# Four weight tiles loaded during the product ahead of a layer norm, and two Newton steps in scalar form

## The chip, the cores and the metric

The kernel runs on one core of one Trainium2 chip. The metric is the device time of one execution in microseconds (us), from start to end on that core; where several executions were taken, their median stands. The core's engines work through instruction queues of their own and meet at semaphores: TensorE (PE; its weight loads are listed as PEld), VectorE (DVE), ScalarE (ACT), GpSimd (POOL), and SyncE (SP), which here only issues DMAs.

## The reference

The program computes a block of a network on 512 tokens of width 1024 and then a second block with a state-space layer and a latent-attention layer. What matters here is the first block:

```python
x = layer_norm(x, ln_emb_g, ln_emb_b)
h = x @ w_in + b_in                      # then two kinds of attention: out_a, out_b
mix = concatenate([out_a, out_b]) @ w_o + b_o
x = layer_norm(DN_ALPHA * x + mix, ln1_g, ln1_b)
ca = memory_cross_attention(x, mem, xa_wq, ..., xa_wo, xa_bo)     # begins with x @ xa_wq
x = layer_norm(DN_ALPHA * x + ca, ln2_g, ln2_b)
f = square(relu(x @ w_up + b_up)) @ w_down + b_down
x = layer_norm(DN_ALPHA * x + f, ln3_g, ln3_b)
```

Everything is float32. A product of float32 accuracy is made of three TensorE products: each operand is split into a high part H and a low part L, and H·H, L·H and H·L are added up.

## The kernel before

Tokens are worked in four tiles of 128 (t = 0 to 3). Weights come in tiles of 128 x 1024 (512 KB). `wload` (L115) handles one: SP issues the DMA into a `wraw` tile, ScalarE copies it into `wh` (L121, the high part), and GpSimd subtracts the two in two halves into `wl` (L124, the low part). All of them lie in one pool, `wp`, with 3 buffers for `wraw` and 5 each for `wh` and `wl`; a buffer is given back when the last instruction that reads it is done.

`gemm_ln` (L559) makes a product and the layer norm behind it. It is called twice: with `w_o` for ln1 and with `xa_wo` for ln2. It opens a pool `lnp` for the norm, which holds gain, bias and small tiles, and runs `gemm_q` (L216): output token-major, in quarters of 256 columns; the first two quarters go over all tokens, the last two are done together, token tile by token tile, with four weight tiles held throughout (L242). After each token tile `ev` runs: L256 adds the residual and sums, L264 and L265 give the mean, L266 (ScalarE) the variance, `nrstd` (L98) one over the standard deviation, L268 and L269 scale and shift. Then the tile is put down (`defer`) for transposing: `xpose` (L272) lets TensorE transpose it (L279), ScalarE write the high part (L145) and VectorE the low part (L146).

`nrstd` starts from ScalarE's square root (L102) and VectorE's reciprocal (L104) and makes one Newton step in two instructions on a single column (L105, L106). It is called 28 times: four times each in the embedding norm, ln1, ln2, ln3 and three RMS norms.

Behind the product stands `gemm_lead` (L170): it loads the first four weight tiles of the next product (`xa_wq` behind ln1, `w_up` behind ln2), takes four PSUM banks and multiplies the first two token tiles (columns 0 to 255) by all four, and then the other two, while the last token tiles are still being normalised and transposed. After it L576 scales the normalised rows on VectorE for the next residual. The remaining tiles of that product are loaded by `gemm_s` through the same `wp` buffers.

The order of the instructions on each engine is not the order of the program text: a planner lists them by program order as priority and by the times at which, on its own model, an instruction's inputs and buffers are ready. On the chip each engine works through its list in order.

Of the kernel before, what the change touches and what calls it, by code (L numbers as in the profile page):

```python
# [8 lines left out]
F32R = mybir.dt.float32r  # L9
AF = mybir.ActivationFunctionType  # L10
ALU = mybir.AluOpType
AX = mybir.AxisListType
P = 128
# [11 lines left out]
class Net:  # L25
# [72 lines left out]
    def nrstd(self, pool, v, n, eps):  # L98
        nc = self.nc
        y = pool.tile([P, 2], F32, tag="nr", name=self.nm("nr"), bufs=4)  # L100
        y0, y1 = y[:, 0:1], y[:, 1:2]
        nc.scalar.activation(y0, v, AF.Sqrt, scale=4.0 / n, bias=self.eps[eps])  # L102
        nc.vector.tensor_scalar(v, v, 4.0 / n, 4.0 * eps, op0=ALU.mult, op1=ALU.add)
        nc.vector.reciprocal(y0, y0)  # L104
        nc.vector.scalar_tensor_tensor(y1, y0, v, y0, op0=ALU.mult, op1=ALU.mult)  # L105
        nc.vector.scalar_tensor_tensor(v, y1, -3.0, y0, op0=ALU.add, op1=ALU.mult)  # L106


    def nbcast(self, pool, key, n, eng=None):
# [2 lines left out]
        return t  # L112


    def wload(self, ap, n=1024, shape=None, leng=None):  # L115
        nc = self.nc
        raw = self.wp.tile([P, 1024], F32, tag="wraw", name=self.nm("wraw"), bufs=3)
        h = self.wp.tile([P, 1024], F32R, tag="wh", name=self.nm("wh"), bufs=5)
        l = self.wp.tile([P, 1024], F32R, tag="wl", name=self.nm("wl"), bufs=5)
        nc.sync.dma_start(raw[:, :n], ap)  # L120
        nc.scalar.activation(h[:, :n], raw[:, :n], AF.Copy)  # L121
        for o in range(0, n, 512):
            e = slice(o, min(n, o + 512))
            (leng or nc.gpsimd).tensor_tensor(l[:, e], raw[:, e], f32(h[:, e]), op=ALU.subtract)  # L124
        return h, l
# [41 lines left out]
            self.flush(n=1)  # L167


    def gemm_lead(self, aps, X, tags):  # L170
        XH, XL = X
        W = [self.wload(ap) for ap in aps]
        pss = [self.bank(tag) for tag in tags]
        for lo in (0, 256):
            q = slice(lo, lo + 256)
            for (wh, wl), ps in zip(W, pss):
                for k in range(8):
                    c = slice(k * P, (k + 1) * P)
                    self.mm3(ps[:, q], wh[:, c], wl[:, c], XH[:, k, q], XL[:, k, q], k == 0, k == 7)
                self.flush(n=1)  # L180
            self.flush()
        return pss


    def gemm_m(self, aps, nk, X, evac, nhs=2, nt=NT, tail=4, leng=None):
        XH, XL = X
        nc2 = nk // 2
        for nh in range(nhs):
# [13 lines left out]
            if tl:  # L202
                W = [self.wload(aps[nh * nc2 + c], leng=leng) for c in range(nc2 - tl, nc2)]
                for t in range(nt):
                    q = slice(t * P, (t + 1) * P)
                    for ci, (wh, wl) in enumerate(W):
                        for kk in range(2):
# [5 lines left out]

    def gemm_q(self, aps, nk, X, evac, tag="mm", tags=()):  # L216
        XH, XL = X
        tags = list(tags)
        bank = lambda: self.bank(tags.pop(0) if tags else tag)
        n4 = nk // 4  # L220
        tq = 2 if nk == 8 else 1

        def part(ps, qs, ts, W):
            first = True
            for y, qn in enumerate(qs):
                for k in range(nk):
                    wh, wl = W[y * n4 + k // 4]
                    n = slice((k % 4) * 256, (k % 4) * 256 + 256)
                    for i, t in enumerate(ts):
                        q = slice(t * P, (t + 1) * P)  # L230
                        o = (y + i) * 256
                        self.mm3(ps[:, o:o + 256], XH[:, k, q], XL[:, k, q], wh[:, n], wl[:, n], first, k == nk - 1)
                        first = False

        for qn in range(4 - tq):
            W = [self.wload(aps[qn * n4 + c]) for c in range(n4)]
            for ts in ((0, 1), (2, 3)):
                ps = bank()
                part(ps, (qn,), ts, W)
                for i, t in enumerate(ts):  # L240
                    evac(t, slice(qn * 256, qn * 256 + 256), ps[:, i * 256:i * 256 + 256], False)
        W = [self.wload(aps[(4 - tq) * n4 + c]) for c in range(tq * n4)]  # L242
        for t in range(NT):
            ps = bank()
            part(ps, range(4 - tq, 4), (t,), W)
            evac(t, slice(D - tq * 256, D), ps[:, :tq * 256], True)
            self.flush(keep=2)
# [42 lines left out]
    def block1(self, dbg):  # L290
        nc, a = self.nc, self.a
# [4 lines left out]
        xt = self.pair(R, [P, 8, T], "xa")  # L296
# [5 lines left out]
        lnp = lp.enter_context(self.pool("lnp"))  # L302
# [5 lines left out]
        W = [wk(0)]  # L308
# [32 lines left out]
        ap = ctx.enter_context(self.pool("attn"))  # L341
# [23 lines left out]
        ap = c3.enter_context(self.pool("small"))  # L365
# [9 lines left out]
        for c, nk in enumerate((3, 3, 2)):  # L375
            wh, wl = self.wload(a["win_m"][:, c * 984:c * 984 + nk * 328], n=nk * 328)
            for kk in range(nk):
                n = slice(kk * 328, (kk + 1) * 328)
# [79 lines left out]
        for n in range(1, NT):  # L458
            w = (n + 1) * P
            q = slice(n * P, (n + 1) * P)  # L460
            sc = scs[n] = tk.tile([P, w], F32, name=f"sc{n}")
            for h in range(8):
                ps = self.mm()
                x = iq[h % 2]
# [34 lines left out]
        mix = self.pair(R, [P, 8, T], "xa")  # L499
# [40 lines left out]
        self.rctx = ExitStack()  # L540
        self.res = self.res_tiles(self.rctx, load=True)
        xt = self.pair(self.Rb, [P, 8, T], "xb")
        self.pre = self.gemm_ln(a["w_o"], 8, mix, "ln1", "xa_bo", xt, lambda: self.gemm_lead([a["xa_wq"][i] for i in range(4)], xt, ("sc", "sc", "pv", "uv")), tags=('mm', 'mm', 'sc', 'sc', 'tr'))
        if self.stop == "ln1":
            for t in range(NT):
                dbg[f"r1_{t}"] = self.res[t]
# [9 lines left out]

    def gemm_ln(self, w, nk, X, ln, nbias, xt, nxt, tags=()):  # L559
        nc = self.nc  # L560
        with self.pool(self.nm("lnp")) as lnp:
            g = self.nbcast(lnp, ln + "_g", D)
            b = self.bcast(lnp, ln + "_b", D)
            bo = self.bcast(lnp, nbias, D)

            def ev(t, cs, ps, last):
                r = self.res[t]
                self.ln_part(lnp, t, r, ps, cs)
                if last:
                    self.ln_finish(lnp, t, r, g, b)  # L570
                    self.defer(lambda: self.xpose(r, xt, t, tag="tr"))
            self.gemm_q([w[i] for i in range(nk)], nk, X, ev, tags=tags)
            pre = nxt()
            if self.stop != ln:
                for r in self.res:
                    nc.vector.scalar_tensor_tensor(r, r, ALPHA, bo, op0=ALU.mult, op1=ALU.add)  # L576
        return pre
# [35 lines left out]
    def block1b(self, dbg):  # L613
        nc, a = self.nc, self.a
# [43 lines left out]
        ao = self.pair(self.Rb, [P, 8, T], "xb")  # L658
# [16 lines left out]
            S = nS  # L675
        ctx.close()
        x2 = self.pair(self.R, [P, 8, T], "xa")
        pre = self.gemm_ln(a["xa_wo"], 8, ao, "ln2", "b_down", x2, lambda: self.gemm_lead([a["w_up"][i] for i in range(4)], x2, ("sc", "sc", "pv", "pv")))
        if self.stop == "ln2":
            for t in range(NT):  # L680
                dbg[f"r2_{t}"] = self.res[t]
# [6 lines left out]
        nw = self.nbcast(fp, "norm_w0", D)  # L688
        u = None
        for hf in range(2):  # L690
# [11 lines left out]
            if hf == 0:  # L702
                self.banks(acc=4, mm=4)
                pre = ()
# [19 lines left out]
        W = self.gate0_w()  # L724
# [917 lines left out]
```

## Time and profile before

| what | us |
|---|---|
| median of 3 runs (lowest to highest) | 1715.33 (1712.84 to 1717.4) |
| profiled execution, its whole time | 1716.78 |
| its span, first to last instruction | 1714.8 |
| TensorE busy in it | 1657.8 (97%) |
| VectorE busy | 913.5 (53%) |
| ScalarE busy | 835.6 (49%) |
| GpSimd busy | 889.2 (52%) |

The shares are averages over very different stages. The granted clock of TensorE is 0.99 of full speed over the span. All times below are from the start of the span of the profiled execution. ln1 lies around 302 to 340, ln2 around 429 to 467, the embedding norm before 48, the third norm around 800 to 835. In a timeline row the first number is the start, the second the duration, `x2` the instructions merged in the row, and the bracket the engine's idle time before it and what ended it.

### The profile page before, as it was taken

How to read it: one execution, taken by the hardware profiler on the slowest of the kernel's cores; microseconds unless marked ns; L12 is line 12 of the kernel's file. 1: busy time of each engine (PE TensorE's matmuls, PEld its weight loads, DVE VectorE, ACT ScalarE, POOL GpSimd, SP SyncE). 2: the span in 40 equal slices, each digit the busy share in tenths (PEclk: the TensorE clock that was granted, in tenths of full speed). 3: DMA queues.
4: the chain of work that ended last, by engine and by line, in shares of the span. 5: the costliest groups of instructions: out<-in, count | busy, mean ns of one | idle time of the engine just before them, and what ended most of it. 6: DMA issues, size and time to landing. Idle time of an engine off the chain costs nothing.

```text
span 1714.8 us, 27158 instructions
## 1 busy us (share of the span) xinstructions
PE 1657.8 (97%) x10203; PEld 1477.9 (86%) x10203; DVE 913.5 (53%) x1965; ACT 835.6 (49%) x1694; POOL 889.2 (52%) x817
## 2 busy tenths in 40 slices
PE   6999999999999999999899999999999999999998
PEld 6877888889988888888878898889999888988998
DVE  7579763743663004402769877779221307667512
ACT  4455664453353124412558777776333426565532
POOL 6756433363374445543556777776544544344431
PEclk9999999999999999999999999999999999999999
DMA  8634313332232222222433333332434442123341
GB/s 286 201 104 130 105 50 114 127 111 78 96 111 98 86 98 93 92 98 78 145 107 99 99 110 100 105 112 86 148 110 136 137 132 66 54 69 97 107 142 50
DMA packets 68178, 187.20 MB, mean 109 GB/s; under 512 B 9968, under 2 KB 16544, under 8 KB 67792
## 3 DMA queue, kind: packets, MB, share of 16 engines
q1 hardware_dynamic: 50128, 152.95, 27.4%
q10 hardware_dynamic: 17632, 30.43, 5.6%
q8 instruction: 80, 1.31, 0.3%
q0 software_dynamic: 288, 2.10, 0.3%
q14 instruction: 50, 0.41, 0.1%
HBM read 163.86 MB, written 14.78 MB: 104 GB/s over the span
## 4 chain that ended last, share of the span: by engine, by line
PE 80%; DVE 10%; issue 3%; ACT 3%; DMA 2%; POOL 1%; ACTq 0%; DVEq 0%; SPq 0%; POOLq 0%
PE mm L129 15%; PE mm L131 15%; PE mm L130 15%; PE acc L130 5%; PE acc L131 5%; PE acc L129 5%; PE sc L130 2%; PE sc L131 2%; PE sc L129 2%; PE pv L130 1%; PE pv L131 1%; PE pv L129 1%; PE tr L887 1%; POOL wl L124 1%; DVE sc L479 1%
## 5 line engine op out<-in xcount | busy, mean ns | idle before, releaser
L124 POOL TENSOR_TENSOR wl<-wraw,wh 128x512 fp32r<-128x512 f32 (+1 forms) x498 | 658.0, 1346 | 509.7 <-ACT wh L121 477.4
L121 ACT ACTIVATE wh<-wraw 128x1024 fp32r<-128x1024 f32 (+4 forms) x254 | 258.5, 1019 | 409.6 <-PE acc L131 123.7
L129 PE MATMUL mm<-xaH,wh 128*128 128x512 f32 x552 | 221.2, 401 | 3.2 <-DVE qbL L140 1.3
L130 PE MATMUL mm<-xaL,wh 128*128 128x512 f32 x552 | 220.4, 399 | 0.0
L131 PE MATMUL mm<-xaH,wl 128*128 128x512 f32 x552 | 220.0, 399 | 0.0
L129 PE MATMUL mm<-wh,xaH 128*128 128x256 f32 x512 | 147.2, 288 | 1.4 <-ACT xaH L145 1.4
L130 PE MATMUL mm<-wl,xaH 128*128 128x256 f32 x512 | 145.6, 284 | 0.0
L131 PE MATMUL mm<-wh,xaL 128*128 128x256 f32 x512 | 145.2, 284 | 0.0
L129 PEld LDWEIGHTS mm<-xaH,wh 128*128 128x128 f32 x552 | 104.4, 189 | 27.2 <-DVE qbL L140 1.8
L131 PEld LDWEIGHTS mm<-xaH,wl 128*128 128x128 f32 x552 | 104.4, 189 | 23.7
L130 PEld LDWEIGHTS mm<-xaL,wh 128*128 128x128 f32 x552 | 104.5, 189 | 23.0
L878 POOL TENSOR_SCALAR S<-S,den 128x128 f32<-128x128 f32 (+1 forms) x96 | 50.9, 534 | 105.1 <-DVE den L877 89.0
L129 PEld LDWEIGHTS mm<-wh,xaH 128*128 128x128 f32 x512 | 97.8, 191 | 2.0 <-ACT xaH L145 1.8
L130 PEld LDWEIGHTS mm<-wl,xaH 128*128 128x128 f32 x512 | 97.7, 191 | 0.2
L131 PEld LDWEIGHTS mm<-wh,xaL 128*128 128x128 f32 x512 | 97.0, 190 | 0.1
L129 PE MATMUL mm<-wh,xbH 128*128 128x256 f32 x336 | 94.9, 283 | 0.7 <-DVE lnsum L256 0.5
L131 PE MATMUL mm<-wh,xbL 128*128 128x256 f32 x336 | 94.4, 284 | 0.1
L130 PE MATMUL mm<-wl,xbH 128*128 128x256 f32 x336 | 94.3, 282 | 0.0
L698 DVE TENSOR_TENSOR rl<-rl 128x512 f32<-128x512 f32 x32 | 43.7, 1366 | 78.4 <-ACT rl L697 78.4
L948 DVE SCALAR_TENSOR_TENSOR xbc<-mm,conv_w,xbc 128x511 f32<-128x511 f32 (+2 forms) x84 | 62.2, 741 | 11.6 <-ACT xbc L946 10.9
L876 ACT ACTIVATE S<-S,mx 128x128 f32<-128x128 f32 (+1 forms) x96 | 53.7, 560 | 24.2 <-DVE mx L875 22.1
L129 PEld LDWEIGHTS mm<-wh,xbH 128*128 128x128 f32 x336 | 63.6, 189 | 1.6 <-DVE lnsum L256 0.7
(633 smaller groups left out, 4747.4 us busy)
## 6 DMA issues: line engine op xcount, KB each, us to landing
wraw<-in_w_up SPq DMA_DIRECT2D x32, 512.0 KB, 3.3
wraw<-in_w_down SPq DMA_DIRECT2D x32, 512.0 KB, 3.2
wraw<-in_ssm_xbc SPq DMA_DIRECT2D x32, 512.0 KB, 3.3
Dm<-acd ACTq DMA_DIRECT2D x32, 256.0 KB, 3.2
wraw<-in_ssm_out SPq DMA_DIRECT2D x16, 512.0 KB, 3.5
wraw<-in_mla_z SPq DMA_DIRECT2D x16, 512.0 KB, 3.5
wraw<-in_mla_out SPq DMA_DIRECT2D x16, 512.0 KB, 3.6
wraw<-in_ssm_z SPq DMA_DIRECT2D x14, 512.0 KB, 3.3
```

The costliest lines, as they stand in the source:

```text
L121: nc.scalar.activation(h[:, :n], raw[:, :n], AF.Copy)
L124: (leng or nc.gpsimd).tensor_tensor(l[:, e], raw[:, e], f32(h[:, e]), op=ALU.subtract)
L129: mm(out, aH, bH, start=first, stop=False, skip_group_check=True)
L130: mm(out, aH, bL, start=False, stop=False, skip_group_check=True)
L131: mm(out, aL, bH, start=False, stop=last, skip_group_check=True)
L479: nc.vector.match_replace(out=scs[n], in_to_replace=m8, in_values=scs[n], imm_value=-3e38)
L698: nc.vector.tensor_tensor(r, r, r, op=ALU.mult)
L876: nc.scalar.activation(s, s, AF.Exp, bias=mx, scale=-1.0, accum_out=den)
L878: nc.gpsimd.tensor_scalar(s, s, den, 1.0, op0=ALU.mult, op1=ALU.mult)
L887: self.nc.tensor.transpose(pt[:, c], S[:, c], self.ident)
L948: nc.vector.scalar_tensor_tensor(o[:, j:], ps[:, :T - j], cw[:, m, 3 - j:4 - j], o[:, j:], op0=ALU.mult, op1=ALU.add)
```

## The change

Four things change. `nrstd`'s two Newton instructions become `tensor_scalar` with two column scalars in place of `scalar_tensor_tensor`. `wload` can take `wh` and `wl` from another pool, with 3 buffers there. `gemm_q` takes a function `ahead` and calls it when the last four weight tiles of its own product have been asked for, ahead of the loop over token tiles. `gemm_ln` passes one that loads the first four tiles of the next product, three of them into the norm's pool and the fourth into `wp`; `gemm_lead` gets them ready made. The arithmetic is the same.

```diff
-        nc.vector.scalar_tensor_tensor(y1, y0, v, y0, op0=ALU.mult, op1=ALU.mult)
-        nc.vector.scalar_tensor_tensor(v, y1, -3.0, y0, op0=ALU.add, op1=ALU.mult)
+        nc.vector.tensor_scalar(y1, y0, v, y0, op0=ALU.mult, op1=ALU.mult)
+        nc.vector.tensor_scalar(v, y1, -3.0, y0, op0=ALU.add, op1=ALU.mult)
...
-    def wload(self, ap, n=1024, shape=None, leng=None):
+    def wload(self, ap, n=1024, leng=None, pool=None):
         nc = self.nc
         raw = self.wp.tile([P, 1024], F32, tag="wraw", name=self.nm("wraw"), bufs=3)
-        h = self.wp.tile([P, 1024], F32R, tag="wh", name=self.nm("wh"), bufs=5)
-        l = self.wp.tile([P, 1024], F32R, tag="wl", name=self.nm("wl"), bufs=5)
+        h, l = ((pool or self.wp).tile([P, 1024], F32R, tag=x, name=self.nm(x), bufs=3 if pool else 5) for x in ("wh", "wl"))
...
-    def gemm_lead(self, aps, X, tags):
+    def gemm_lead(self, aps, X, tags, W=None):
         XH, XL = X
-        W = [self.wload(ap) for ap in aps]
+        W = W or [self.wload(ap) for ap in aps]
...
-    def gemm_q(self, aps, nk, X, evac, tag="mm", tags=()):
+    def gemm_q(self, aps, nk, X, evac, tag="mm", tags=(), ahead=None):
...
         W = [self.wload(aps[(4 - tq) * n4 + c]) for c in range(tq * n4)]
+        if ahead:
+            ahead()
         for t in range(NT):
...
-    def gemm_ln(self, w, nk, X, ln, nbias, xt, nxt, tags=()):
+    def gemm_ln(self, w, nk, X, ln, nbias, xt, nw, lead, tags=()):
...
-            self.gemm_q([w[i] for i in range(nk)], nk, X, ev, tags=tags)
-            pre = nxt()
+            W = []
+            self.gemm_q([w[i] for i in range(nk)], nk, X, ev, tags=tags, ahead=lambda: W.extend(self.wload(nw[i], pool=lnp if i < 3 else None) for i in range(4)))
+            pre = self.gemm_lead(None, xt, lead, W)
```

The two calls of `gemm_ln` pass the weights (`a["xa_wq"]`, `a["w_up"]`) and the bank tags in place of the function that called `gemm_lead`.

## Rows read from the trace of the kernel before

**Rows 1.** The page: busy time, share of the span and instructions.
```profile
PE 1657.8 (97%) x10203; PEld 1477.9 (86%) x10203; DVE 913.5 (53%) x1965; ACT 835.6 (49%) x1694; POOL 889.2 (52%) x817
```

**Rows 2.** TensorE's waits, whole span: who, released by: us in total, times, longest.
```profile
PE mm L279 <- DVE res L330: 4.7, 2, 4.4
PE sc L130 <- DVE xbL L146: 4.0, 1, 4.0
...
PE sc L130 <- DVE lnmu L264: 2.7, 1, 2.7
...
PE z L131 <- DVE lnmu L265: 1.2, 1, 1.2
```

**Rows 3.** Windows: length, busy PE, PEld, DVE, ACT, POOL, granted clock, DMA share, GB/s.
```profile
318.00:323.20 5.20, 0.96 (x6) 0.55 (x4) 5.20 (x9) 1.49 (x3) 5.20 (x4) 0.99 0.61 202
323.20:326.40 3.20, 3.17 (x15) 3.17 (x16) 3.20 (x3) 1.79 (x4) 2.06 (x3) 0.50 0.49 163
...
452.80:456.10 3.30, 3.30 (x18) 3.30 (x17) 3.27 (x5) 1.54 (x3) 3.30 (x3) 0.50 0.43 159
```

**Rows 4.** Timeline of VectorE behind ln1.
```profile
310.75 0.69 DVE L256 CUSTOM_DVE_ANT_0 res<-mm,res 128x512 f32<-128x512 f32 x1 [0.62 <-PE mm L131]
...
313.02 1.22 DVE L576 SCALAR_TENSOR_TENSOR res<-res,xa_bo 128x1024 f32<-128x1024 f32 x1
...
317.38 0.69 DVE L256 CUSTOM_DVE_ANT_0 res<-mm,res 128x512 f32<-128x512 f32 x1 [0.62 <-PE mm L131]
...
317.99 1.10 DVE L105 SCALAR_TENSOR_TENSOR nr<-nr,lnvar 128x1 f32<-128x1 f32 x1
...
319.08 2.29 DVE L576 SCALAR_TENSOR_TENSOR res<-res,xa_bo 128x1024 f32<-128x1024 f32 x1
321.30 1.21 DVE L106 SCALAR_TENSOR_TENSOR lnvar<-nr 128x1 f32<-128x1 f32 x1
322.44 0.14 DVE L265 TENSOR_SCALAR lnmu<-lnmu 128x1 f32<-128x1 f32 x1
322.50 1.27 DVE L146 TENSOR_TENSOR xbL<-tr,xbH 128x512 fp32r<-128x512 f32 x2
```

**Rows 5.** Timeline of GpSimd around ln1.
```profile
296.41 5.04 POOL L124 TENSOR_TENSOR wl<-wraw,wh 128x512 fp32r<-128x512 f32 x4 [1.54 <-ACT wh L121]
...
315.12 8.62 POOL L124 TENSOR_TENSOR wl<-wraw,wh 128x512 fp32r<-128x512 f32 x6 [12.65 <-ACT wh L121]
```

**Rows 6.** Timeline of ScalarE behind ln1.
```profile
317.81 1.09 ACT L145 ACTIVATE xbH<-tr 128x512 fp32r<-128x512 f32 x2 [0.70 <-PE tr L279]
```

**Rows 7.** Timeline of VectorE behind ln2.
```profile
446.58 2.30 DVE L268 SCALAR_TENSOR_TENSOR res<-res,lnmu,ln_g 128x1024 f32<-128x1024 f32 x1 [2.48 <-ACT jk L266]
...
449.55 1.54 DVE L576 SCALAR_TENSOR_TENSOR res<-res,b_down 128x1024 f32<-128x1024 f32 x1
451.01 0.68 DVE L146 TENSOR_TENSOR xaL<-tr,xaH 128x512 fp32r<-128x512 f32 x1
```

**Rows 8.** Timeline of ScalarE around ln2.
```profile
442.87 1.06 ACT L121 ACTIVATE wh<-wraw 128x1024 fp32r<-128x1024 f32 x1 [0.79 <-PE mm L131]
```

**Rows 9.** Timeline of GpSimd around ln2.
```profile
444.01 12.90 POOL L124 TENSOR_TENSOR wl<-wraw,wh 128x512 fp32r<-128x512 f32 x8 [17.08 <-ACT wh L121]
```

**Rows 10.** Timeline of VectorE in the embedding norm.
```profile
24.52 1.24 DVE L105 SCALAR_TENSOR_TENSOR nr<-nr,mv 128x1 f32<-128x1 f32 x1
...
30.41 2.28 DVE L330 SCALAR_TENSOR_TENSOR res<-res,mv,ln_emb_b 128x1024 f32<-128x1024 f32 x1
```

**Rows 11.** Timeline of VectorE in the third norm.
```profile
818.47 1.31 DVE L105 SCALAR_TENSOR_TENSOR nr<-nr,lnvar 128x1 f32<-128x1 f32 x1
819.71 0.68 DVE L146 TENSOR_TENSOR xaL<-mm,xaH 128x512 fp32r<-128x512 f32 x1
```

**Rows 12.** Instructions on the tile lnvar: duration ns min/median/max, first and last start.
```profile
L105 DVE SCALAR_TENSOR_TENSOR nr<-nr,lnvar x12: 210/220/1315, 307.1 to 826.3; 128x1 f32<-128x1 f32 x12
...
L269 DVE SCALAR_TENSOR_TENSOR res<-res,lnvar,ln_b x12: 1269/1284/2367, 307.5 to 827.8; 128x1024 f32<-128x1024 f32 x12
```

More of the change, by code (lines that the diff above doesn't have):

```diff
@@ L542, in block1 @@
         xt = self.pair(self.Rb, [P, 8, T], "xb")
-        self.pre = self.gemm_ln(a["w_o"], 8, mix, "ln1", "xa_bo", xt, lambda: self.gemm_lead([a["xa_wq"][i] for i in range(4)], xt, ("sc", "sc", "pv", "uv")), tags=('mm', 'mm', 'sc', 'sc', 'tr'))
+        self.pre = self.gemm_ln(a["w_o"], 8, mix, "ln1", "xa_bo", xt, a["xa_wq"], ("sc", "sc", "pv", "uv"), tags=('mm', 'mm', 'sc', 'sc', 'tr'))
         if self.stop == "ln1":
@@ L677, in block1b @@
         x2 = self.pair(self.R, [P, 8, T], "xa")
-        pre = self.gemm_ln(a["xa_wo"], 8, ao, "ln2", "b_down", x2, lambda: self.gemm_lead([a["w_up"][i] for i in range(4)], x2, ("sc", "sc", "pv", "pv")))
+        pre = self.gemm_ln(a["xa_wo"], 8, ao, "ln2", "b_down", x2, a["w_up"], ("sc", "sc", "pv", "pv"))
         if self.stop == "ln2":
```

## The prediction

> **What bounds the kernel now.** I read the page first: TensorE is busy for 97% of the span [rows 1], so only what shortens its pauses, or the stretches in which it runs at half clock, can move the end. The list of its waits names the pauses that this change can reach [rows 2]: 4.4 us in the embedding norm, until L330 has written a token tile; 4.0 us behind the first layer norm (ln1) and 2.7 us behind the second (ln2), both until L146 has written the low half of the second token tile, which the first products read; 1.2 us in the third norm. (The last two rows name L264 and L265, one-element steps that stand next to L146 on VectorE; it is L146 that TensorE needs.) The windows then show that the pauses behind ln1 and ln2 are each followed by some 3.2 us at a granted clock of 0.50, 1.2 instead of 2.4 GHz [rows 3]; half of that, 1.6 us, is lost as well.
>
> Why is L146 late? Behind ln1 ScalarE writes its half from 317.81 on, the first of two parts by 318.4 [rows 6], so L146 could begin there. It begins at 322.50 [rows 4]. In between VectorE runs L105, one element per partition, in 1.10 us instead of 0.22 [rows 12]; L576 in 2.29 us instead of the 1.22 of the one at 313.02; L106, again one element, in 1.21; and L265, 0.14 us. All this time GpSimd splits weights without a break [rows 5]. The row of L265 is the telling one: a TENSOR_SCALAR of one element is not held up, a SCALAR_TENSOR_TENSOR of one element is held up for about one GpSimd instruction, and so is the big one. L146 itself, with one operand in PSUM, isn't: 1.27 us for two. Behind ln2 the same queue stands with other members: L268 at 2.30 us and L576 at 1.54 us ahead of L146, and no Newton step [rows 7].
>
> **The Newton steps (L105, L106)**, 28 calls. Unhindered, L105 falls from 0.22 to about 0.14 us, the length of L265; in nearly all calls that lies under TensorE's products. On the path stands the last call of all: -0.1 us. Four places where a step was held up count.
> Embedding norm: L105 at 24.52 takes 1.24 us and delays what follows it by 1.1; L330, at the end of the chain, runs 2.28 us from 30.41 [rows 10]. Begun 1.1 us earlier it may also meet GpSimd at a better moment, so TensorE gains between 0 and 1.6 us; but GpSimd's splits then wait for VectorE in turn and feed the next products, so I take -1.0.
> Behind ln1: L105 and L106 ahead of L146 lose 0.95 and 1.06 us, so L146 comes 2.0 us earlier, other things equal.
> Behind ln2: none stands ahead of L146: 0.
> Third norm: an L105 of 1.31 us stands ahead of the second L146 at 819.71 [rows 11]; TensorE's pause there, 1.2 us, can go. But GpSimd's queue of splits is not shorter for it: the next large VectorE instruction meets the split that the small one met before. Between 0 and -1.4; I take -0.6.
> The one-element TENSOR_SCALAR in the rows has constants for its scalars [rows 4]; one with columns in memory does not occur, so this is the nearest row, and the old hold of up to 1.1 us stays as the other bound. The Trainium skill, SBUF — State Buffer, section "Who interferes with whom", counts tensor_scalar among the operations that can take the port pair shared with GpSimd, in a two-port mode, besides instructions with two SBUF inputs. By that the new form could wait as the old one does, and this part would bring 0; the row of L265, 0.14 us with GpSimd busy, speaks against it for one element.
>
> **The four weight tiles.** Each is one DMA on SP's queue, one ScalarE copy (L121, 1.06 us [rows 8]) and two GpSimd subtractions (L124; 5.04 us for four, so 1.26 each [rows 5]). None of this is removed. The order on SP's queue stays: the product's tiles, then these four. Before, one of the four found a free buffer; the other three waited until the product gave its last buffers back, which is why ScalarE copies the second tile behind ln2 at 442.87, released by a product, L131 [rows 8]. With three tiles in the norm's pool that wait is gone, and they can be split in the 12.65 us (ln1) and 17.08 us (ln2) in which GpSimd stood idle [rows 5, 9]; the 7.6 us of six subtractions fit there.
> Was TensorE waiting for these weights? No: neither of its long waits behind the two norms names L121 or L124 [rows 2]. So the move brings nothing by itself. Its use would be an idle GpSimd while VectorE prepares L146. Here I had to choose. The buffers that the product gives back during its last token tile are now free for the *next* weights of the following product, and the planner refills a buffer as soon as it and a landed tile are there: before, eight subtractions ran in one go behind ln2, four tiles, one more than the three that were waiting [rows 9]. So I expect the fifth to seventh tile to be split just where the second to fourth were, and L576, L268 and L269 to be held up as before.
> What the move adds is hold-ups earlier. Ahead of L576 at 313.02 VectorE runs L268 and L269 for the first two token tiles, four two-input instructions of 1.28 us. One that meets a split is held up by 1.0 us (2.30 against 1.28 [rows 7, 12]). VectorE has 0.62 us idle twice to absorb it [rows 4]. All four met: 4 x 1.0 - 1.24 = +2.8 us; none: 0. I take three: +1.8. Against the 2.0 of the Newton steps ln1 comes out at -0.2. Its bounds: the pause gone (322.50 back to 318.4, -4.1) with the clock's -1.6, and +2.8.
> Behind ln2 the early splits lie in the idle 17.08 us before 444.01, and VectorE has 2.48 us idle before its critical queue [rows 7], which covers two meetings. So 0; with that cover gone +1.5 at most, and -2.7 - 1.6 if the pause goes.
> ScalarE's queue is the other place to look at: the copies now stand, in order, ahead of the norm's L266 of the first tiles, and a copy that waits for its DMA holds L266 and with it L268. The first two token tiles have time to spare, since TensorE transposes each of them a whole tile's product later: 0, bound +1.4 (one L121 and a piece of a landing). On GpSimd's queue L111, which L268 needs, is issued first. The 24 KB more in the norm's pool lie on tiles that the attention has left, and what comes to lie on them later is written after the first products' last read: 0.
>
> **The sum.** -0.1 - 1.0 - 0.2 + 0 - 0.6 = -1.9 us. The profiled execution took 1716.78 us, 1714.8 of it span; that would be 1712.9 of span and 1714.9 in all. On the median of 1715.33, which is what is compared, it is 1713.4 us, 0.11% less. Under 0.3%, 5.1 us, a measurement of this kernel can hardly tell a change from none.
>
> **The rivals.**
> *The gap closes (faster).* If the freed buffers are refilled later, GpSimd is idle while L146 is due. Behind ln1 L105, L576, L106 and L265 then take 1.7 us in place of 4.5 (-2.8), behind ln2 L268 and L576 take 1.28 + 1.22 in place of 2.30 + 1.54 (-1.3), and the clock may stay at 1.00 (2 x -1.6). With the other terms' -1.7 that is -9.0: 1706.3 us; with L576 behind L146 it would go down to 1703.6. For it: the held-up instructions are there in the rows. Against it: the fourth tile in one go [rows 9]. Chance 0.20. Half of it, 2.0 behind ln1 and no fall of the clock there, is 2.0 + 1.6 + 1.7 = 5.3 less, 1710.0 us; chance 0.15.
> *A longer queue on VectorE (slower).* The early splits meet all four instructions of the first two tiles, the freed buffers are refilled at once, and VectorE comes late to its critical queue; it decides from a backlog over the 2.0 us that the Newton steps give back. With ln1 at +2.8 and its 2.0 spent on new meetings, ScalarE's wait at +1.4, ln2 at +1.5 and one more stretch at the low clock, +1.6, less 1.7, it is +5.6: 1720.9 us. For it: from 318 to 326.4 VectorE does not pause at all [rows 3]. Against it: the idle spots before, and an early start of the splits. Chance 0.12.
> *The new form waits too.* Then the Newton terms are gone and ln1 stays at +1.8: 1717.1 us, within 0.3%. Chance 0.08.
>
> **How the numbers follow.** My own case has 0.45, at 1713.4, from 1710.5 to 1717.5. Within 0.3% are it and the last rival: 0.53. Faster by over 0.3%: 0.20 + 0.15 = 0.35. Slower: 0.12. The two outer cases reach beyond their times; 1703.5 to 1720.0 leaves out some 0.08 below and 0.11 above.
>
> **What would show it.** Right: L105 and L106 as TENSOR_SCALAR at about 0.14 us even where GpSimd is busy; the second to fourth tile's L121 ahead of the second token tile's L266; GpSimd still splitting when the last token tile's L256 ends; a pause of 3 to 5 us behind ln1 and of about 2.7 us behind ln2, each with 0.50 after it; the pause at L330 about 1 us shorter. Wrong: GpSimd idle in those two places and L146 right behind L145 (the first rival); L268 or L269 of the first two tiles at 2.3 us and L146 behind ln1 over 5 us after the last L256 (the second); L105 over 0.5 us anywhere (the third). The planner also orders every queue anew; if VectorE's order behind the norms changes, say L576 behind L146, the terms no longer hold.

## The result, and the profile after

| kernel | median us (lowest to highest, runs) | against before, 95% interval |
|---|---|---|
| before | 1715.26 (1712.84 to 1717.68, 6) | |
| changed | 1732.15 (1727.6 to 1732.64, 6) | 1.0091 [1.008, 1.0101] |

The change makes the kernel slower by 0.91%, 16.9 us; the prediction was 1713.4 us, 0.11% faster. The profiled execution took 1731.1 us, 1729.1 of it span, 14.3 more than before. Line numbers move by one or two: L121 is L120 now, L124 L123, L145 and L146 L144 and L145, L256 L257, L268 and L269 L269 and L270, L576 L578.

The page of the changed kernel: busy time by engine. TensorE is busy 7.5 us longer for the same number of instructions [rows 1], as it runs longer at half clock (the windows below); the other half of the loss is pauses.

```profile
PE 1665.3 (96%) x10203; PEld 1484.1 (86%) x10203; DVE 909.1 (53%) x1965; ACT 835.9 (48%) x1694; POOL 896.8 (52%) x817
```

The list of TensorE's waits in the changed kernel: who, released by what, us in total, times, longest.

```profile
PE tr L280 <- DVE xbL L145: 5.1, 1, 5.1
PE sc L129 <- DVE lnmu L265: 4.3, 2, 2.7
PE mm L128 <- DVE xaL L139: 4.2, 1, 4.2
PE mm L280 <- DVE res L331: 3.5, 2, 2.9
...
PE py L1051 <- DVE y L1068: 2.1, 1, 2.1
```

Three of these are new against [rows 2]: the first (ahead of the second token tile's transposes, ln1), the third (behind the first products of ln1) and the last (state-space stage). The pause in the embedding norm fell from 4.4 to 2.9 us, though in `e5_first_in_wp` below, with the same Newton form, it is 4.6; the one behind ln2 is still 2.7; the one behind ln1 is 1.6 now, with the 5.1 ahead of it.

Windows of the changed kernel (columns as in [rows 3]): the new pause at ln1, what follows it, the new pause behind the first products, what follows it, and the stretch behind ln2.

```profile
314.20:319.50 5.30, 0.27 (x3) 0.06 (x1) 5.30 (x5) 2.34 (x4) 5.24 (x3) 0.95 0.39 138
318.90:329.10 10.20, 7.97 (x35) 7.47 (x36) 9.48 (x20) 3.68 (x6) 6.19 (x5) 0.50 0.44 154
...
350.40:354.80 4.40, 0.28 (x3) 0.07 (x1) 2.12 (x3) 4.15 (x6) 3.02 (x2) 0.80 0.00 0
353.10:359.90 6.80, 5.05 (x12) 3.99 (x13) 5.15 (x7) 3.86 (x6) 2.16 (x1) 0.50 0.54 184
458.90:465.70 6.80, 5.69 (x26) 5.69 (x27) 6.69 (x13) 1.76 (x4) 6.80 (x4) 0.50 0.43 154
```

Before, ln1 had 3.2 us at 0.50 [rows 3], and there was nothing at 350 (a window of the kernel before, same columns):

```profile
345.00:360.00 15.00, 15.00 (x82) 12.84 (x81) 7.88 (x7) 7.61 (x10) 13.37 (x9) 1.00 0.57 185
```

Cut at the last TensorE instruction ahead of pauses that these kernels share, the span compares like this (the third column is the kernel with the Newton steps alone, below):

| stretch, up to | before | changed | Newton alone |
|---|---|---|---|
| the pause at xaH ahead of ln1's product | 291.0 | 288.2 | 287.2 |
| the first wait for S in the cross attention | 86.7 | 97.9 | 84.6 |
| the pause behind ln2 | 71.0 | 71.0 | 71.0 |
| the wait for dts, start of the state-space stage | 407.0 | 407.7 | 407.9 |
| the wait for X in that stage | 319.5 | 324.4 | 319.2 |
| the end of the span | 539.6 | 540.1 | 539.2 |

The sum is +14.3, and two rows carry it: +11.2 from ln1 to the cross attention, +4.9 in a stage that the change doesn't touch. ln2, the other place with early tiles, shows nothing.

What happens at ln1. GpSimd and VectorE of the changed kernel, timelines:

```profile
301.53 20.86 POOL L123 TENSOR_TENSOR wl<-wraw,wh 128x512 fp32r<-128x512 f32 x12 [3.49 <-DMA wraw<-in_xa_wq]
```
```profile
303.14 2.02 DVE L269 SCALAR_TENSOR_TENSOR res<-res,lnmu,ln_g 128x1024 f32<-128x1024 f32 x1
...
306.33 2.32 DVE L270 SCALAR_TENSOR_TENSOR res<-res,lnvar,ln_b 128x1024 f32<-128x1024 f32 x1
308.58 2.31 DVE L269 SCALAR_TENSOR_TENSOR res<-res,lnmu,ln_g 128x1024 f32<-128x1024 f32 x1
...
311.55 0.26 DVE L105 TENSOR_SCALAR nr<-nr,lnvar 128x1 f32<-128x1 f32 x1
...
312.10 2.28 DVE L270 SCALAR_TENSOR_TENSOR res<-res,lnvar,ln_b 128x1024 f32<-128x1024 f32 x1
314.30 2.29 DVE L578 SCALAR_TENSOR_TENSOR res<-res,xa_bo 128x1024 f32<-128x1024 f32 x1
316.51 2.28 DVE L269 SCALAR_TENSOR_TENSOR res<-res,lnmu,ln_g 128x1024 f32<-128x1024 f32 x1
318.72 1.27 DVE L145 TENSOR_TENSOR xbL<-tr,xbH 128x512 fp32r<-128x512 f32 x2
```

GpSimd, which before stood idle for 12.65 us here [rows 5], now runs twelve subtractions in one piece, and each of VectorE's six large instructions with two SBUF operands meets one: 2.02 to 2.32 us instead of 1.28. From the first L269 to L145 of the *first* token tile, at 318.72, it takes 15.6 us; before, the same six took 9.7, from 305.61 to 315.35 (VectorE of the kernel before, the first of the six and the low half of the first token tile):

```profile
305.61 1.28 DVE L268 SCALAR_TENSOR_TENSOR res<-res,lnmu,ln_g 128x1024 f32<-128x1024 f32 x1
...
315.35 1.28 DVE L146 TENSOR_TENSOR xbL<-tr,xbH 128x512 fp32r<-128x512 f32 x2
```

L145 has to read the two PSUM banks of that tile before TensorE can transpose the second tile into them. So TensorE stops not behind the first products, where the prediction looked, but ahead of the transposes.

What happens at 350. ScalarE and SP's queue of the changed kernel:

```profile
350.65 1.06 ACT L120 ACTIVATE wh<-wraw 128x1024 fp32r<-128x1024 f32 x1 [12.37 <-PE uv L129]
351.61 1.04 ACT L144 ACTIVATE xcH<-kvraw 128x1024 fp32r<-128x1024 f32 x1
352.56 1.25 ACT L138 ACTIVATE xaH<-sc,xa_bq 128x512 fp32r<-128x512 f32 x2
```
```profile
319.95 6.24 SPq L119 DMA_DIRECT2D wraw<-in_xa_wo  x3
328.19 2.30 SPq L623 DMA_DIRECT2D kvraw<-kd  x2
```

The four first products end one after another in four PSUM banks; each could be evacuated (L138, L139) when it is done. But ScalarE idles 12.37 us: at the head of its queue stands a weight copy, L120, of `xa_wo`, the product *after the next*. Its raw tile was fetched from 319.95 on, and it waits for the buffer that the last of the four first products (`uv`) reads. All four evacuations stand behind it, and the next product needs the banks and what is written from them: 4.2 us of pause, and 6.8 us at half clock that begin inside it.

### The profile page after: what moved, and what is told of

Same layout as the page of the kernel before. It is cut to its first block, busy times and chain, and to the rows that moved or that the text cites. A ratio compares the mean times of both kernels' runs of the same rounds, so it can differ in the third digit from the quotient of the medians.

```text
span 1729.1 us, 27155 instructions
## 1 busy us (share of the span) xinstructions
PE 1665.3 (96%) x10203; PEld 1484.1 (86%) x10203; DVE 909.1 (53%) x1965; ACT 835.9 (48%) x1694; POOL 896.8 (52%) x817
## 4 chain that ended last, share of the span: by engine, by line
PE 78%; DVE 13%; ACT 3%; issue 2%; DMA 2%; POOL 1%; ACTq 0%; DVEq 0%; SPq 0%; POOLq 0%
PE mm L128 14%; PE mm L129 14%; PE mm L130 14%; PE acc L129 5%; PE acc L130 5%; PE acc L128 5%; PE sc L129 2%; PE sc L130 2%; PE sc L128 2%; PE pv L129 2%; PE pv L130 1%; PE pv L128 1%; DVE xbc L950 1%; DVE sc L480 1%; DVE m L479 1%
## 5 line engine op out<-in xcount | busy, mean ns | idle before, releaser
L123 POOL TENSOR_TENSOR wl<-wraw,wh 128x512 fp32r<-128x512 f32 (+1 forms) x498 | 666.2, 1363 | 523.3 <-ACT wh L120 490.6
L120 ACT ACTIVATE wh<-wraw 128x1024 fp32r<-128x1024 f32 (+4 forms) x254 | 258.7, 1019 | 419.5 <-PE acc L130 125.7
L130 PEld LDWEIGHTS mm<-wh,xaL 128*128 128x128 f32 x512 | 97.9, 192 | 0.1
```

What stands on the lines that cost most here:

```text
L130: mm(out, aL, bH, start=False, stop=last, skip_group_check=True)
```

## The experiments

All ratios are against the kernel before, run beside each group on the same chip; the medians of before were 1715.62, 1715.30, 1717.11 and 1717.31 us for the four groups in order.

### One part alone

The first four kernels take the change apart. `e1_newton` is the kernel before with the two tensor_scalar lines. `e2_move` is the change with

```diff
-        nc.vector.tensor_scalar(y1, y0, v, y0, op0=ALU.mult, op1=ALU.mult)
-        nc.vector.tensor_scalar(v, y1, -3.0, y0, op0=ALU.add, op1=ALU.mult)
+        nc.vector.scalar_tensor_tensor(y1, y0, v, y0, op0=ALU.mult, op1=ALU.mult)
+        nc.vector.scalar_tensor_tensor(v, y1, -3.0, y0, op0=ALU.add, op1=ALU.mult)
```

`e3_ln1` and `e4_ln2` pass `ahead` only for the one norm, and load the four tiles in `gemm_lead` for the other:

```diff
-self.gemm_q(..., ahead=lambda: W.extend(...))
+self.gemm_q(..., ahead=lambda: W.extend(...) if ln == "ln1" else None)
-pre = self.gemm_lead(None, xt, lead, W)
+pre = self.gemm_lead([nw[i] for i in range(4)], xt, lead, W)
```

> The kernel before with the two Newton steps in scalar form and nothing else. Theory A (the splits that are now early hold up VectorE's queue at ln1; the Newton form is a small gain): in the changed kernel the work ahead of ln1 came 2.9 us earlier, and L105 and L106 behind ln1 lost 2.0 us before; so 2 to 5 us less than before, 1710 to 1713.5 us. Rival B (the loss is that of an order that the planner makes anew, whatever is edited): the stretch behind ln2, which this edit touches no more than the whole change does, shows the +5 us that it lost in the changed kernel, and the time is 1717 to 1721 us. Rival C (one-element tensor_scalar with column scalars, 0.26 us in place of 0.22, costs): within 1 us of 1715.3.

> The change with the old form of the Newton steps: the four weight tiles alone are moved. Theory A: the whole loss and what the Newton form had given back, 1733 to 1737 us; L105 and L106 at 1.1 to 2.3 us each where GpSimd splits without a break behind ln1. Rival C: 1730 to 1732 us, no worse than the whole change.

> The whole change at ln1, the four tiles loaded as before at ln2. Theory A: ln1 lost 11.2 us up to the first products of ln2, ln2 about 1, and the rest of the loss came further on; so 1722 to 1728 us, with a TensorE pause of about 5 us ahead of the transposes of the second token tile and one of about 4 us behind the first products. Rival B: what is lost further on (5 us between 864 and 1189 us) hangs on the planner's order and not on ln2, so it is there too or has another sign: 1728 to 1733 or under 1720 us.

> The whole change at ln2, the four tiles loaded as before at ln1. Theory A: ln1 keeps only the gain of the Newton steps (2 to 5 us less), ln2 adds 0 to 2 us, the longer stretch at half clock behind it 1.7: 1712 to 1717 us. Rival B: the 5 us of the later stretch stay: 1717 to 1722 us.

| kernel | median us | ratio, 95% interval |
|---|---|---|
| e1_newton | 1713.27 | 0.9982 [0.9969, 0.9996] |
| e2_move | 1726.71 | 1.0069 [1.0046, 1.0092] |
| e3_ln1 | 1730.22 | 1.009 [1.0064, 1.0115] |
| e4_ln2 | 1713.66 | 0.9991 [0.9977, 1.0004] |

The Newton steps are a small gain, the tiles at ln1 the whole loss, the tiles at ln2 about 0.1%, within the error. `e3_ln1` is 2 us above what theory A gave, and where rival B put it, since the loss of the state-space stage came with it (324.8 us) though ln2 is as before. `e2_move` missed both of its ranges: the move without the Newton steps should have been slower than the whole change, and is faster by about 5 us. Its stretch from ln1 to the cross attention is nearly as long as the whole change's (96.9 us); the difference lies in the state-space stage, 317.0 us against 324.4. That belongs to the last part of this section.

How fine the stretches can be read is shown by `e3_ln1` too. From ln1 to the cross attention it runs the same instructions in the same order as the changed kernel, on TensorE, VectorE, ScalarE and GpSimd, and takes 95.6 us where that one takes 97.9: its pause ahead of the transposes is 4.3 us, not 5.1, and behind the pause of 4.2 us it runs 3.4 us at half clock, not 6.8. Each stretch is from one execution, so a difference of some 2 us between two of them can be chance.

Behind ln1, `e1_newton` shows the queue that the prediction had in mind for the Newton term (VectorE's timeline; in this kernel the old line numbers hold):

```profile
314.14 0.27 DVE L105 TENSOR_SCALAR nr<-nr,lnvar 128x1 f32<-128x1 f32 x1
...
314.40 2.02 DVE L576 SCALAR_TENSOR_TENSOR res<-res,xa_bo 128x1024 f32<-128x1024 f32 x1
316.34 0.20 DVE L106 TENSOR_SCALAR lnvar<-nr 128x1 f32<-128x1 f32 x1
316.46 0.68 DVE L146 TENSOR_TENSOR xbL<-tr,xbH 128x512 fp32r<-128x512 f32 x1
```

L146 starts 2.3 us after L105 instead of 4.5 [rows 4]. What is left of the queue is L576.

### The early splits

`e8_no_split` leaves out GpSimd's subtractions for the four tiles at ln1; DMAs, copies and buffers stay. `e6_early` keeps them but asks for three of the tiles one quarter of the product earlier:

```diff
         for qn in range(4 - tq):
+            if ahead and qn:
+                ahead()
             W = [self.wload(aps[qn * n4 + c]) for c in range(n4)]
```

> The whole change, but the four tiles at ln1 are not split: no subtraction on GpSimd for them, and the products read the high part in place of the low part. Their DMAs, ScalarE copies and buffers stay, so the output isn't the reference's. Theory A1: with GpSimd's eight subtractions away, L269 and L270 of the first two token tiles take 1.28 us and the pause ahead of the second token tile's transposes goes; 5 to 9 us less than the changed kernel, 1723 to 1727 us. Rival (ScalarE's copies, in order ahead of the norm's square, are what makes VectorE late): the pause of 4 us and more stays, 1730 us and over.

> The whole change, with three tiles asked for one quarter earlier (ahead of the second quarter of the product, where VectorE does little) and the fourth behind the product, in the common pool. Theory A1 (the splits beside the norm of the first two token tiles cost the 5 us ahead of the second token tile's transposes): GpSimd is idle again from about 302 to 315 us, L269 and L270 of the first two tiles take 1.28 us, and the pause ahead of the transposes goes: 5.2 us and half of the 6.8 us more at half clock; the pause at 350 stays: 1721 to 1725 us. Rival (the three buffers more, not the splits' place, cost: the tiles that are refilled run beside the norm in any case): a pause of 4 us and more ahead of those transposes stays, 1729 us and over.

`e8_no_split`: 1724.46 us, 1.0047 [1.0031, 1.0064], as theory A1 had it. GpSimd (the first row: its timeline) is idle again as before, and the pause ahead of the transposes is gone; VectorE's L272, the L270 of the change, takes 1.29 us in the middle case (second row: the instructions on the tile res from 301 to 326 us, ns as minimum, median and maximum).

```profile
312.95 13.57 POOL L125 TENSOR_TENSOR wl<-wraw,wh 128x512 fp32r<-128x512 f32 x7 [13.10 <-ACT wh L120]
```
```profile
L272 DVE SCALAR_TENSOR_TENSOR res<-res,lnvar,ln_b x3: 1285/1286/2103, 307.7 to 321.0; 128x1024 f32<-128x1024 f32 x3
```

The copies are all there, so ScalarE's copies are not what makes VectorE late; the splits are. The stretch falls from 97.9 to 89.0 us. The pause of 4.3 us behind the first products stays, as it should.

`e6_early`: 1750.53 us, 1.0201 [1.0183, 1.0219], a miss by 25 us. The pause ahead of the transposes is gone here too, but its list of TensorE's waits has two new ones, both at the second quarter of a product, of ln1's and of ln2's:

```profile
PE sc L128 <- ACT wh L120: 10.5, 1, 10.5
...
PE mm L128 <- ACT wh L120: 6.8, 1, 6.8
```

The early tiles take the three `wraw` buffers and the queues ahead of the product's own weights. The expectation had counted only where the splits run, not the loads that they push back.

### The copy at the head of ScalarE's queue

`e5_first_in_wp` puts the first of the four tiles, not the fourth, into the common pool (`pool=lnp if i else None`), so that the buffer comes free three products earlier. `e9_hold` keeps the change and puts a holder between: one buffer of the weight pool is taken by an instruction that can only run once the fourth bank is evacuated, so no copy of `xa_wo` can stand ahead of the evacuations.

```diff
         ao = self.pair(self.Rb, [P, 8, T], "xb")
+        hold = self.wp.tile([P, 1024], F32R, tag="wh", name=self.nm("wh"), bufs=5)
+        nc.scalar.activation(hold[:, 0:2], f32(qT[0][:, 3, 0:2]), AF.Copy)
```

> The whole change, with the first of the four tiles in the common pool and the other three in the norm's pool (changed kernel: the fourth in the common pool). Theory A2 (the pause of 4.3 us behind the first products of ln1 comes from ScalarE's queue: a copy of a later weight tile waits there for the buffer that the last of the first products gives back, and the evacuation of the four banks stands behind it): the buffer now comes free with the first of these products, the pause at 350 goes, and the 6.8 us at half clock behind it: 1722 to 1727 us. Rival (the evacuation is late because VectorE and GpSimd are behind by what ln1 lost): the pause stays, over 3 us, 1730 to 1733 us.

> The whole change, and one tile of the weight pool is taken, ahead of the weights of the product after next, by an instruction of two elements that reads the fourth evacuated bank: no copy of those weights can then stand ahead of the evacuations in ScalarE's queue. Theory A2 (narrowed: what the freed buffers let come early is the loading of xa_wo, the product after next; its DMAs and copies wait for buffers at the head of SP's and ScalarE's queues, and the k/v loads and the evacuations stand behind them): the pause at 350 falls below 1.5 us and the half clock behind it goes: 1723 to 1728 us. Rival (VectorE and the k/v data are late by themselves): the pause stays over 3 us, 1730 to 1734 us.

`e5_first_in_wp`: 1732.38 us, 1.0087 [1.0062, 1.0112]: no gain, and the pause is 6.6 us. The copy does start earlier, but now the same thing happens one queue back (ScalarE, then SP's queue):

```profile
344.76 1.06 ACT L120 ACTIVATE wh<-wraw 128x1024 fp32r<-128x1024 f32 x1 [5.72 <-PE sc L129]
344.78 0.33 ACTq L71 DMA_DIRECT2D xa_bq<-in_xa_bq  x1
355.00 1.06 ACT L144 ACTIVATE xcH<-kvraw 128x1024 fp32r<-128x1024 f32 x1 [9.18 <-DMA kvraw<-kd]
```
```profile
321.62 27.16 SPq L119 DMA_DIRECT2D wraw<-in_xa_wo  x4
348.87 1.44 SPq L623 DMA_DIRECT2D kvraw<-kd  x2
```

A fourth load of `xa_wo` waits at the head of SP's queue for a raw buffer until 348.45; the loads of k and v stand behind it, ScalarE's L144 waits for them, and the evacuations stand behind L144. So the theory was too narrow: it is not this one buffer, it is that loads for the product after next come early in two in-order queues. The time and the pause are those that the rival gave, with another cause: if VectorE and GpSimd were late by themselves, the holder of `e9_hold` could not help, and it does. The expectation for `e9_hold` says so.

`e9_hold`: 1715.82 us, 0.9999 [0.9989, 1.0009]. The kernel with one instruction of two elements more has lost nothing against the one before: it takes back 16 us, against 4 to 9 expected. Not all of that is the queue's. ScalarE goes from the k/v copy to each bank as it is done, and there is no pause at 350:

```profile
337.93 1.06 ACT L144 ACTIVATE xcH<-kvraw 128x1024 fp32r<-128x1024 f32 x1 [1.59 <-DVE res L578]
342.13 0.69 ACT L138 ACTIVATE xaH<-sc,xa_bq 128x512 fp32r<-128x512 f32 x1 [3.15 <-PE sc L130]
343.44 0.69 ACT L138 ACTIVATE xaH<-sc,xa_bq 128x512 fp32r<-128x512 f32 x1 [0.62 <-PE sc L130]
```

The stretch from ln1 to the cross attention falls from 97.9 to 89.8 us, by 8.1: the 4.2 of pause, half of 6.8 at half clock, and 0.7 by which the pause ahead of the transposes, which is still there, is shorter (4.3 us). Against `e3_ln1` it falls by 5.8, and without the splits (`e8_no_split`, and `e10_hold_no_split` below) the same holder brings 6.1; so the queue is worth some 6 to 8 us. Another 4.5 of the 16 come from the state-space stage, 319.9 us against 324.4, which the holder has no part in but through the planner's order.

### Both at once

`e7_both` has the earlier loading of `e6_early` and the pool of `e5_first_in_wp`. `e10_hold_no_split` has the holder and no splits of the early tiles at ln1.

> Both of the two edits: the second to fourth tile in the norm's pool one quarter earlier, the first in the common pool behind the product. Theories A1 and A2 together: ln1 as in the kernel with the Newton steps alone, 1711 to 1717 us, and below 1711 if GpSimd, with three splits out of the way, leaves VectorE free while L145's low half of the second token tile is due. Rival B (the planner's order of the later stages decides): 1718 us and over with a pause under 2.5 us behind ln1.

> The same with the four tiles at ln1 not split at all (the products read the high part in place of the low part, so the output isn't the reference's). Theories A1 and A2: neither of the two pauses is left up to 360 us; what is then over the kernel with the Newton steps alone (1713.3 us) is the later order: 1715 to 1719 us with the slow order of the state-space stage (some 325 us from its first product's wait to the wait at X), 1710 to 1714 with the other (some 319). Rival (copies, DMAs and buffers cost in their own way): 1720 us and over.

`e7_both`: 1748.65 us, 1.019 [1.017, 1.0209], a miss by more than 30 us; it inherits what made each of its parts fail, waits for the product's own weights of 9.4 and 7.0 us, and 5.4 us behind the first products. `e10_hold_no_split`: 1713.3 us, 0.9976 [0.9966, 0.9986], inside the expectation and level with the Newton steps alone. Its stretch is 82.9 us, so without the splits it is 6.9 us shorter than `e9_hold`'s 89.8. Splits and queue together account for 15.0 of the 97.9 us, more than the change added (13.3 over `e1_newton`); that fits splits which had cost something in the kernel before already, but 1.7 us is within what two stretches can differ by.

### Is the move any good with its costs undone?

`e11_bo_late` goes the other way: no early tiles, Newton steps, and the bias that L576 adds loaded behind the last token tile into the buffer `jk`, so that L576 can't stand ahead of L146. `e12_hold_bo` is the whole change with the holder and the same late bias.

```diff
-            bo = self.bcast(lnp, nbias, D)
...
             pre = nxt()
+            bo = self.bcast(lnp, nbias, D, tag="jk")
```

> The kernel before with the Newton steps in scalar form, and the bias that L576 adds is loaded behind the norm's last token tile, into the buffer of the norm's squares, so that L576 cannot stand ahead of the low half of the second token tile on VectorE. If L576 is the last thing that holds up that half (2.29 us at ln1, 1.54 at ln2 in the kernel before), the pause of 2.0 us at ln1 and most of the 2.9 us at ln2 go, and the half clock behind ln2 too: 1706 to 1711 us. Rival (the chain of L268, Newton and L269 of the next token tile takes its place in the queue, or GpSimd's splits hold it up as well): 1712 to 1715 us.

> The whole change with two things undone that cost around it: the held weight tile (no copy of xa_wo's weights ahead of the evacuations) and the bias of L578 loaded behind the last token tile. What is left of the change is the early splits themselves, against the kernel with Newton steps and late bias (1709.1 us). Theory A1 (early splits hold up L269 and L270 of the first token tiles): a pause of 2 to 4 us ahead of the second token tile's transposes is left, though L578's 2.30 us is out of the queue ahead of it: 1710 to 1715 us. Rival (with L578 out of the way the early splits pay, since GpSimd's queue is shorter while the low half of the second token tile is due): no pause over 1 us at either norm, 1704 to 1709 us.

`e11_bo_late`: 1709.07 us, 0.9955 [0.9941, 0.997], faster than both kernels. VectorE goes from the last L256 straight to L146, and L576 comes when its bias has landed; neither norm is followed by a drop of the clock (windows behind ln1 and ln2):

```profile
314.42 0.68 DVE L256 CUSTOM_DVE_ANT_0 res<-mm,res 128x512 f32<-128x512 f32 x1
...
315.03 1.28 DVE L146 TENSOR_TENSOR xbL<-tr,xbH 128x512 fp32r<-128x512 f32 x2
...
322.84 1.23 DVE L576 SCALAR_TENSOR_TENSOR res<-res,xa_bo 128x1024 f32<-128x1024 f32 x1 [0.99 <-DMA xa_bo<-in_xa_bo]
```
```profile
315.60:319.00 3.40, 3.24 (x27) 3.24 (x28) 2.06 (x5) 2.41 (x4) 3.40 (x4) 1.00 0.45 155
442.00:445.50 3.50, 3.35 (x28) 3.35 (x29) 1.59 (x4) 2.94 (x5) 3.50 (x4) 1.00 0.46 150
```

`e12_hold_bo`: 1710.12 us, 0.9957 [0.9943, 0.9972]. With L578 out of the way the early splits still hold up L269 and L270 (2.28 us at 311.63, as in the changed kernel), but the wait ahead of the transposes is only 1.5 us. The ratio is that of `e11_bo_late` within the error: with these two costs out of the way, the four early weight tiles neither help nor hurt. Neither theory is borne out in full: the time lies in theory A1's range but the pause is smaller than the one expected, and there is no gain as the other has it.

### The state-space stage

No run was made for this term alone; it comes out of the others. The order of VectorE's instructions in that stage, read from the traces, is the same, instruction by instruction, in the kernel before, `e1`, `e2`, `e4`, `e5`, `e6`, `e9`, `e10`, `e11` and `e12`; the changed kernel, `e3` and `e8` share another, which differs in 215 of 400 places (and TensorE's in 848 of 1959). `e7` has a third order, without that wait for X, and is left out here. From the wait for dts to the wait for X the ten take 317.0 to 320.6 us, the three 324.4, 324.8 and 326.5. Windows over that stretch, the changed kernel and then `e9_hold`:

```profile
864.70:1189.00 324.30, 315.14 (x1961) 281.31 (x1960) 252.61 (x399) 228.06 (x493) 227.66 (x194) 0.98 0.31 102
```
```profile
855.00:1174.90 319.90, 312.02 (x1961) 279.05 (x1960) 248.07 (x400) 228.65 (x495) 227.60 (x196) 0.98 0.33 104
```

The same 1961 matmuls, 3.1 us more TensorE time and 1.3 more of pauses; the wait for y at L1068 (2.1 us) is in those three kernels only. So the planner had listed a stage 550 us further on in another order, and that order costs 4 to 5 us (324.4 against 319.5 before and 319.9 in `e9_hold`). That the order goes with the time is shown by thirteen kernels; which of the exchanged instructions costs it, and what in ln1 tips the planner, was not tried and stays open.

## Why the prediction was wrong, point by point

**The Newton steps** came out near their size: the sum gave -3.7 us, and alone they measure -0.18% [-0.31, -0.04], some 3 us. Behind ln1 the stretch is 2.1 us shorter (84.6 against 86.7), where the step said 2.0; L105 and L106 are no longer held up there, but 2 us is also what two stretches can differ by. Two sizes were off: the new L105 and L106 take 0.27 and 0.21 us, not 0.14 (below), and the gain of 0.6 in the third norm did not come: TensorE's longest pause there is 2.9 us in `e1_newton`, where it was 1.2, and from ln2 to the state-space stage it is 0.9 us longer. How much of the gain lies in the embedding norm is not settled: up to the pause ahead of ln1's product the kernels with the new form (those that load a quarter earlier left aside) need 286.7 to 290.6 us, the one with the old form and the moved tiles 288.7, the kernel before 291.0. The rival that the new form waits too is ruled out.

**The early splits, ln1: the step that failed first.** The prediction counted four instructions that a split could meet, took three of them, and set idle spots of VectorE against them: +1.8 us, at most +2.8. Six were met, about 1.0 us each; L578 and the third tile's L269 are the two that the count left out, though they stand ahead of the first tile's L145 in both kernels. Of the two idle spots that were set against them, only the one at 310.75 lies ahead of that low half, which began at 315.35. And the backlog was carried to the wrong place: the prediction followed it to the low half of the second token tile, with the time to spare of a whole tile's product, and didn't look at the first tile's L145, which TensorE needs to get its transposition banks back. In place of +1.8 stand 5.2 us (89.8 of `e9_hold` less 84.6 of `e1_newton`), good to some 2 us; the splits as a whole, with the old ones that they replace, are worth 6.9 with the holder and 8.9 without it.

**The freed buffers.** That they are refilled at once was right, and the prediction used it for GpSimd only. The same refilling goes one step further: the three extra buffers let the loads run on into `xa_wo`, and those loads and copies wait at the head of SP's and ScalarE's queues. The term *ScalarE's queue* stood at 0 with a bound of +1.4 because it looked only at the copies beside the norm, and never at who is queued behind the copies after it. It is worth some 6 to 8 us. The list of waits of the kernel before can't show this, as there the loads of k and the first of v were issued ahead of any of `xa_wo` (its first at 345.42); the step would have been to write down, for each queue, what the extra buffers let in ahead of what.

**ln2: 0** was right, in pause and time (71.0 against 71.0). GpSimd had its free stretch, and the same two instructions as in [rows 7] meet the refill (GpSimd, then VectorE of the changed kernel):

```profile
452.28 11.67 POOL L123 TENSOR_TENSOR wl<-wraw,wh 128x512 fp32r<-128x512 f32 x7 [16.11 <-ACT wh L120]
```
```profile
454.85 2.29 DVE L269 SCALAR_TENSOR_TENSOR res<-res,lnmu,ln_g 128x1024 f32<-128x1024 f32 x1 [1.68 <-ACT jk L267]
...
457.82 1.54 DVE L578 SCALAR_TENSOR_TENSOR res<-res,b_down 128x1024 f32<-128x1024 f32 x1
```

The stretch at half clock behind it is 6.8 us here, 3.3 before. That this is the early tiles' doing is not shown: `e9_hold`, which has them too, ran 3.4 us at half clock there, and `e1_newton`, which hasn't, none after a pause of the same 2.7 us.

**The planner's order** had a closing sentence and no term. It cost 4.9 us in a stage that no step mentions; by itself it would have turned the forecast of -1.9 us into a loss of 3.0.

**The rivals.** *A longer queue on VectorE* has the right sign, two of its conditions came true (all four instructions met, buffers refilled at once), and L268 and L269 at 2.3 us were named as its mark. The other half of the mark, the low half of the second token tile over 5 us after the last L256, did not come (320.05 to 323.39), since TensorE's wait had moved to the first tile. Its 1720.9 us is still 11 us short, for ScalarE's queue and the planner's order. It deserved more than 0.12: the row that decided it, a VectorE without any pause behind ln1 [rows 3], was read and set aside for the idle spots ahead of it, which together were 1.2 us.

**The sum as measured**, against the kernel before in the profiled executions: -2.9 up to ln1's product, -2.1 Newton behind ln1, +5.2 early splits, +8.1 ScalarE's queue, +4.9 the order of the state-space stage, +1.1 in the rest: +14.3. The split of the 13.3 us between splits and queue is good to some 2 us.

## What to carry to other kernels

A buffer more doesn't only let in the load that it was added for; it lets in everything behind that load too. Before adding one, write down for each in-order queue (SP, ScalarE) what will now be issued early, what it will wait for at the head of the queue, and who stands behind it; one instruction that takes a buffer until the urgent work is done removed that wait here. And where two engines hold each other up, count every instruction up to the first result that the bound engine needs, not only those ahead of the wait that the profile names today; taking a single movable instruction (here L576) out of that queue gained some 4 us beyond the Newton steps (0.9955 against 0.9982), where moving all the weights lost.

## What the runs showed of the hardware

A one-element TENSOR_SCALAR with two column scalars takes 0.26 to 0.27 us (L105) and 0.20 to 0.22 (L106), a little more than the unhindered old form (0.22 and 0.16), and was never held up beside GpSimd; L105 of the old form went up to 1.32 us [rows 12]. Instructions on the tile lnvar in the changed kernel, ns as minimum, median and maximum:

```profile
L105 DVE TENSOR_SCALAR nr<-nr,lnvar x12: 258/270/274, 305.8 to 835.2; 128x1 f32<-128x1 f32 x12
L106 DVE TENSOR_SCALAR lnvar<-nr x12: 198/214/215, 306.1 to 835.5; 128x1 f32<-128x1 f32 x12
```

The prediction weighed what the Trainium skill says in SBUF — State Buffer, "Who interferes with whom": tensor_scalar is among the operations that can enter a two-port mode and then contend with GpSimd, when its operands meet that mode's conditions. At one element no run here shows it. The same section of the Trainium skill says that a VectorE instruction with two SBUF inputs contends with a GpSimd instruction that reads SBUF; all six large ones at ln1 agree, at 2.02 to 2.32 us in place of 1.28.

The clock's price is not one figure per pause. Behind ln2 TensorE waited 2.7 us in the kernel before, in the changed kernel and in `e1_newton`; at a granted 0.50 it then ran 3.3, 6.8 and 0 us (`e1_newton`, the window behind that pause):

```profile
446.00:449.50 3.50, 3.50 (x31) 3.50 (x31) 3.46 (x6) 1.54 (x3) 3.50 (x3) 1.00 0.46 150
```

Behind ln1 the changed kernel ran 10.2 us at 0.50, from just before the end of its 5.1 us of waiting on and with the 1.6 us inside. In `e11_bo_late`, which waits at most 1.5 us at one place there, the clock stayed at 1.00 behind both norms; but a short wait is no safeguard: in the attention ahead of ln1 a wait of 1.2 us, in the kernel before up to 207.45, came with half clock from 207.0 to 213.8 there and with none in `e1_newton` and `e11_bo_late`.
